# Queries and keys of two of three attention groups as block products, in a two-layer hybrid decoder on one NeuronCore

## The chip, the cores and the metric

The kernel runs on one core of one Trainium2 chip. Its time is the device time of one launch in microseconds, the median of several runs. The engines of a core work side by side, each through its own queue: TensorE (PE; its weight loads are listed apart as PEld), VectorE (DVE), ScalarE (ACT), GpSimd (POOL) and SyncE (SP), which here only issues DMAs. A change is compared with the kernel before on the same chip.

## What is computed

Two layers, each with a token mixer and an FFN, on 512 tokens of width 1024, all in float32. The mixer's input projection gives, among much else, queries, keys and values of 18 attention heads in three groups of six, with windows and dilations of their own. Cut to what matters:

```python
def _hybrid_mixer(x, rel_bias, w_in, b_in, w_attn_proj, w_ret_proj, w_out):
    z = jnp.einsum('bsd,dc->bsc', x, w_in) + b_in
    q_a, k_a, v_a, q_r, k_r, v_r, g_r, gate_a, gate_b = jnp.split(z, SPLIT_POINTS, axis=-1)
    ...
    for gi, (window, dilation) in enumerate(ATTN_GROUPS):   # (128,1), (512,4), (2048,16)
        o, lse = _dilated_window_attention(q_a[:, :, gi], k_a[:, :, gi], v_a[:, :, gi], ...)
    wts = jax.nn.softmax(jnp.stack(lses, axis=0), axis=0)
    y_a = jnp.sum(wts[..., None] * jnp.stack(outs, axis=0), axis=0)
    y_r = _retention(...)
    y_b = jax.nn.silu(g_r) * y_r
    merged = (sigmoid(gate_a) * (y_a @ w_attn_proj) + sigmoid(gate_b) * (y_b @ w_ret_proj))
    return merged @ w_out
```

The columns of `w_in` that matter here are those of q and k, 128 at a time: one column group holds two heads of one attention group.

## The kernel before

**Products.** A float32 operand is split into a high and a low part (`hilo`, or `high`/`low` in `Right`): ACT casts the loaded weights to the high part, DVE subtracts to get the low part. A product is then three matmuls (`mm3`, line 85): high by high, low by high, high by low. All matmuls of projections have line 83.

**Plain projections.** `wstat` (247) computes 128 output columns for all 512 tokens: 8 pieces of the contraction by 3 matmuls of 512 columns, with weights as the stationary operand. `pair_units` (215) loads the weights of q and k for one column group in two halves of the contraction, two DMAs each, into one raw buffer of 128 x 1024 a half; `unit` (114) makes the high and low parts.

**Block products.** `wide` (420) computes a two-by-two block product with seven products in place of eight. Columns (two output blocks), contraction and tokens are halved: product i of `ORDER` takes one block or one sum of blocks of x (`x_left`, sums S1 to S4 made once a layer) and one block or sum of blocks of the weights: B11, B12, B21, B22 and P1 = B11 + B12, P2 = P1 + B22, P3 = B12 + B22, P4 = P1 + B21. `Right` (322) loads the blocks and makes the operands: P1 and P3 are made before the change by a DMA of POOL that adds to the loaded block (`accum_op`), P2 and P4 by DVE in P1's buffer (361). The order `WIDE` is 1 (B11), 5 (P1), 6 (P2), 2 (B21), 7 (P3), 3 (B22), 4 (P4). One product is 2 x 4 x 3 = 24 matmuls of 256 columns. Results gather in three PSUM chains: A over products 1, 6, 7, 4; C over 5 and 3; X for 2. The function `ev` gets each finished chain. Rotary, the gates and the FFN use `wide`.

**Operands ahead.** Raw loads have 8 buffers, high and low parts 4 each (`wp`), PSUM 8 banks, the working tiles `w2` 6. The cast of the next product's operand is issued ahead of the present product's matmuls. Within an engine's queue the instructions are ordered at compile time by a planner that takes the next one that its model holds to be ready, in the order in which the program is written where several are; a wait that is longer in fact than in the model holds up what is queued behind it.

**Work beside.** The attention of a lot (`attention_pair`, 531) is a list of small operations: for 8 blocks `scores` (PE, then DVE and ACT for the softmax), `turn` (PE transposes, ACT copies) and `values` (PE, ACT copies), then `swap` and a tail that weighs the groups against each other. These lie in the queue `side`. `tick` (148) is called behind every three projection matmuls and takes entries from it at the rate that `pace` sets; `drain` runs what is left. `nothing` is an empty entry that sets the distance.

**The stage of the change.** Six heads a group make three lots of two heads, `hp` = 0, 1, 2 (line 900). Lot zero's queries and keys come at the layer's start. For lots one and two, lines 901 to 907 project q and k of groups 0, 1 and 2 one after the other (six `wstat`, `qk_put` on DVE adds the bias and scales), while the attention of the lot before is taken from `side` with `pace(32)`. The attention of the last lot runs beside the first rotary projection, a `wide` (line 922). In each layer the stage runs twice, so four times in all. For groups 1 and 2 the tiles `qk` are written with tokens permuted by four (`p (l r) -> p r l`).

Of the kernel before, what the change touches and what calls it, by code (L numbers as in the profile page):

```python
# [11 lines left out]
F32 = mybir.dt.float32  # L12
F32R = mybir.dt.float32r
I32 = mybir.dt.int32
AF = mybir.ActivationFunctionType
ALU = mybir.AluOpType
# [3 lines left out]
P = 128  # L20
# [5 lines left out]
HD = 64  # L26
HPG = 6
NG = 3
GW = HPG * HD
AW = NG * GW  # L30
# [7 lines left out]
C_QA, C_KA, C_VA = 0, AW, 2 * AW  # L38
# [16 lines left out]
def hybrid_kernel(ctx, tc, x, rel_bias, w_in, b_in, w_attn_proj, w_ret_proj, w_out,  # L55
                  ln1_g, ln1_b, w_ffn_gate, w_ffn_up, w_ffn_down, ln2_g, ln2_b,
                  c_cos, c_sin, c_dec, c_hot, c_id, out):
    nc = tc.nc
    pe, act, dve, pool = nc.tensor, nc.scalar, nc.vector, nc.gpsimd
# [4 lines left out]
    sm = ctx.enter_context(tc.tile_pool(name="sm", bufs=4, side="right"))  # L64
# [20 lines left out]
    def mm3(ps, ah, al, bh, bl, start, stop):  # L85
        mm(ps, ah, bh, start, False)
        mm(ps, ah, bl, False, False)
        mm(ps, al, bh, False, stop)

    def psum(name="px"):  # L90
        return psm.tile([P, S], F32, tag="mm", name=name)
# [5 lines left out]
    def raw(name="raw"):  # L97
        return rawp.tile([P, 1024], F32, tag="raw", name=name)

    def work(name):  # L100
        return wk.tile([P, S], F32, tag="w2", name=name)

    def rows(w):
        return w.rearrange("(k p) c -> p k c", p=P)

    def view(t, a, b):
        return t[:, :a * b].rearrange("p (a b) -> p a b", a=a)

    def load(src, a, b):
        v = view(raw(), a, b)  # L110
        nc.sync.dma_start(v, src)
        return v

    def unit(v):
        a, b = v.shape[1], v.shape[2]
        h = view(wp.tile([P, 1024], F32R, tag="whi", name="whi"), a, b)
        l = view(wp.tile([P, 1024], F32R, tag="wlo", name="wlo"), a, b)
        hilo(v, h, l)
        return h, l
# [26 lines left out]
    side, rate, credit, awaited = deque(), [1.0], [0.0], [0] * NI  # L146

    def tick(us):

        if side:  # L150
            credit[0] += rate[0] * us
            while side and credit[0] >= 1.0:
                credit[0] -= 1.0
                side.popleft()()

    def pace(us):
        rate[0], credit[0] = len(side) / us, 0.0

    def drain():
        while side:  # L160
            side.popleft()()
# [4 lines left out]
    def need(*tiles):  # L166

        while any(awaited[i] for i in tiles):
            side.popleft()()
# [72 lines left out]
    def part_of(us, k, q):  # L242
        h, l = us[k // 4]
        cs = slice(q * P, (q + 1) * P)
        return h[:, k % 4, cs], l[:, k % 4, cs]

    def wstat(us, q):

        need(*range(NI))
        ps = psum("ps")  # L250
        for k in range(KD):
            h, l = part_of(us, k, q)
            mm3(ps, h, l, xh[:, k], xl[:, k], k == 0, k == KD - 1)
            tick(STEP)
        return ps
# [41 lines left out]
    def tail_units(raws):  # L297

        out_ = []
        for j, r in enumerate(raws):  # L300
# [12 lines left out]
    ORDER = ((1, "A11", "B11"), (2, "A12", "B21"), (5, "S1", "P1"), (3, "S4", "B22"),  # L313
             (6, "S2", "P2"), (7, "S3", "P3"), (4, "A22", "P4"))
    CHAIN = {1: "A", 6: "A", 7: "A", 4: "A", 2: "X", 5: "C", 3: "C"}
    FIRST = (1, 2, 5)
    WIDE = tuple(ORDER[i] for i in (0, 2, 4, 1, 5, 3, 6))
    WIDE1 = tuple(ORDER[i] for i in (0, 1, 2, 4, 3, 5, 6))

    class Right:  # L320
# [1 line left out]

        def __init__(self, src, shapes, order=ORDER, loads=("B11", "B21", "P1", "P3", "B22")):
            self.src, self.shapes, self.order, self.loads, self.t = src, shapes, order, loads, {}

        def load(self, *names):
            for n in names:
                if (n, 0) in self.t:  # L330
                    continue
                for u, (a, b) in enumerate(self.shapes):
                    r = self.t[n, u] = load(self.src({"P1": "B11", "P3": "B12"}.get(n, n), u), a, b)
                    if n in ("P1", "P3"):
                        pool.dma_start(r, self.src({"P1": "B12", "P3": "B22"}[n], u), accum_op=ALU.add)  # L335
# [18 lines left out]
        def begin(self, n):  # L354

            if n == "B11":
                self.load(*self.loads)
            elif n in ("P2", "P4"):
                for u in range(len(self.shapes)):
                    r = self.t["P1", u]  # L360
                    dve.tensor_tensor(out=r, in0=r, in1=self.t["B22" if n == "P2" else "B21", u], op=ALU.add)  # L361
            return self.high(n)
# [57 lines left out]
    def wide(right, left, ev):  # L420


        ps = {}
        for (i, an, bn), ((h, l),) in zip(right.order, right.operands()):
            c = CHAIN[i]
            if i in FIRST:
                ps[c] = psum("ps")
            for q in range(2):
                cs = slice(q * P, (q + 1) * P)
                for k in range(4):  # L430
                    ah, al = left(an, k, slice(0, 256))
                    mm3(ps[c][:, q * 256:(q + 1) * 256], h[:, k, cs], l[:, k, cs], ah, al,
                        i in FIRST and q == 0 and k == 0, k == 3)
                    tick(STEP / 2)
            ev(i, ps[c])
# [217 lines left out]

    VB = 288

    bTs = []
    for ly in range(DEPTH):
        bTs.append(sm.tile([P, COLS // P], F32, tag="bT", name="bT", bufs=2))

    def bias_cols(ly, braw):  # L660
        n = COLS // P
        px = psum()
        pe.transpose(px[:, :n], braw, ident[:n, :n])
        dve.tensor_copy(bTs[ly], px[:, :n])

    def layer(ly, cp):
        w_l = rows(w_in[ly])
        b_l = b_in[ly]
        bT = bTs[ly]

        def bcol(c):
            return bT[:, c // P:c // P + 1]
# [74 lines left out]
        with stage("attn") as ap_, stage("attw", 4) as aw:  # L747
            qk = {}

            def qk_slot(hp, g):  # L750
                qk[hp, g] = opp.tile([P, 2, S], F32, tag="op", name="qk")

            def qk_units(hp, g, how=pair_units):
                c = g * GW + hp * P
                return how(w_l, C_QA + c, C_KA + c)

            def qk_put(hp, g, j, ps):
                cc = (C_QA, C_KA)[j] + g * GW + hp * P
                o_, i_ = qk[hp, g][:, j], ps
                if g:  # L760
                    o_ = o_.rearrange("p (r l) -> p r l", r=4)
                    i_ = i_.rearrange("p (l r) -> p r l", r=4)
                dve.tensor_scalar(o_, i_, bcol(cc), (HD ** -0.5, 1.0)[j], op0=ALU.add, op1=ALU.mult)

            if ly == 0:
                x0 = [slot("x0", F32) for _ in range(NI)]
# [2 lines left out]
                px = psum()  # L769
# [16 lines left out]
                for hf in range(2):  # L786
                    for i in range(2):
                        load_x(i, hf)
                    for g, j in tiles:
                        c = (C_QA, C_KA)[j] + g * GW  # L790
# [11 lines left out]
                ops = [to_xT(x0[i].rearrange("p a b -> p (a b)"), i, cp, late) for i in range(NI)]  # L802
# [52 lines left out]
            for t in range(2):  # L855
                c1, c2 = C_VA + t * VB, C_VA + (2 + t) * VB

                def put(i, s, c):
                    nc.sync.dma_start(v_d[i * P:(i + 1) * P, c - C_VA:c - C_VA + VB], s)
# [23 lines left out]
            def load_v(hp):  # L883
                v = [ap_.tile([P, NG, P], F32, tag="v", name="v", bufs=6) for _ in range(NI)]
                for i in range(NI):
                    c = hp * P
                    nc.sync.dma_start(v[i][:, 0], v_d[i * P:(i + 1) * P, c:c + P])
                    vr = v_d[:, GW:].rearrange("(l r) (g e) -> r l g e", r=4, g=2)[i]
                    nc.sync.dma_start(v[i][:, 1:], vr[:, :, c:c + P])
                return v  # L890
# [7 lines left out]
            bias, tail = {}, []  # L898
            load_bias(0)
            for hp in range(HPG // 2):  # L900
                if hp:
                    for g in range(NG):
                        us = qk_units(hp, g)
                        qk_slot(hp, g)
                        for j in range(2):
                            qk_put(hp, g, j, wstat(us, j))
                    drain()
                ops, t_ = attention_pair(hp, [qk[hp, g] for g in range(NG)], load_v(hp), outputs_last if hp == HPG // 2 - 1 else outputs_, bias, yaT)
                if hp + 1 < HPG // 2:
                    ops.insert(17, lambda hp=hp: load_bias(hp + 1))  # L910
                if hp == 0:
                    pool.dma_start(cos, c_cos)
                    pool.dma_start(sin, c_sin)
                for at, f in zip((30, 29, 27, 19, 17, 15, 13, 12, 3), reversed(tail)):
                    ops.insert(at, f)
                side.extend([nothing] * (3 if hp < 2 else 8) + ops)
                tail = t_
                pace(32)
            n = [nothing]
# [8 lines left out]
        with stage("ret") as rp:  # L928
# [57 lines left out]
            for h in range(RH):  # L986
# [7 lines left out]
                ops = ret_scores(h)  # L994
# [7 lines left out]
                ops, turns = ret_outputs(h)  # L1002
# [65 lines left out]
            for dp in range(KD // 2):  # L1068
                h, l = was[dp]
# [5 lines left out]
                for e in range(2):  # L1075
                    cs = slice(e * P, (e + 1) * P)
                    ps = psum("ps")
                    for t in range(NG):
                        mm3(ps, h[:, t, cs], l[:, t, cs], ya[t][:, 0], ya[t][:, 1], t == 0, t == NG - 1)
                    v = sgs[dp][:, e]  # L1080
# [36 lines left out]
        with stage("mp") as mp:  # L1117
# [10 lines left out]
            for dp in range(KD // 2):  # L1128
# [9 lines left out]
                for hh, (h, l) in enumerate(us):  # L1138
                    for e in range(2):
                        cs = slice(e * P, (e + 1) * P)  # L1140
                        for t in range(4):
                            k = 4 * hh + t
# [166 lines left out]
```

## Time and profile before

| | us |
|---|---|
| median of 3 runs | 2157.8 |
| lowest and highest | 2156.14, 2160.75 |
| the profiled run | 2158.48 |
| span of the profiled run, first to last instruction | 2156.7 |

The granted clock of TensorE is 0.999 over the span. The profiled run lies 0.7 us above the median, and its span 1.8 us below its time. Where the stage lies in the first layer: the last `qk_put` of lot zero is at 47.8 us, those of lot one lie between 101.0 and 144.1, those of lot two between 150.2 and 195.1; in the second layer, lots one and two lie between 1170.9 and 1265.3. All busy shares are busy time over the span, and a matmul that drains counts as busy, so starts must be compared to see TensorE's pace.

### The profile page before, as it was taken

To read this page: it belongs to the slowest core of one execution; us is meant where nothing else is said; L and a number is where in the kernel's file an instruction comes from. 1 tells how busy PE (TensorE), PEld (TensorE's weight loads), DVE (VectorE), ACT (ScalarE), POOL (GpSimd) and SP (SyncE) were. 2 spreads that over 40 slices of the span, in tenths; PEclk is the share of its full clock that TensorE was granted. 3 is DMA by queue.
4 is the path that set the end of the run, shared out by engine and by line. 5 is a ranking of instruction groups with operands and counts; after the bars stand their busy time and mean duration, and the time that the engine had idled before them with its cause. 6 is when DMAs were issued, how large, how long until landed. Compare 5 with 4: busy or idle time off the path is not lost.

```text
span 2156.7 us, 33739 instructions
## 1 busy us (share of the span) xinstructions
PE 2141.0 (99%) x13482; PEld 1896.2 (88%) x13482; DVE 1448.5 (67%) x2077; ACT 1016.2 (47%) x1573; POOL 237.9 (11%) x249
## 2 busy tenths in 40 slices
PE   9999999999999999999999999999999999999998
PEld 8977888889988899989898788888899889999996
DVE  6635897887744776747675367887867357666575
ACT  4544554655623353525245455555666233444350
POOL 5011101011000101000120111111010001010001
PEclk9999999999999999999999999999999999999999
DMA  8854458577776266656269444667777662666551
GB/s 260 241 135 102 115 146 209 157 183 176 227 266 202 63 169 145 167 128 165 72 175 250 107 112 118 155 173 192 175 187 249 229 195 59 179 144 168 123 159 39
DMA packets 317629, 351.25 MB, mean 163 GB/s; under 512 B 22173, under 2 KB 255809, under 8 KB 317344
## 3 DMA queue, kind: packets, MB, share of 16 engines
q1 hardware_dynamic: 231936, 253.01, 38.0%
q0 software_dynamic: 58256, 83.29, 21.0%
q10 hardware_dynamic: 27280, 12.80, 2.1%
q8 instruction: 105, 1.72, 0.3%
q14 instruction: 52, 0.43, 0.1%
HBM read 323.26 MB, written 28.53 MB: 163 GB/s over the span
## 4 chain that ended last, share of the span: by engine, by line
PE 92%; issue 4%; DMA 2%; DVE 1%; ACT 1%; POOL 1%; SPq 0%; POOLq 0%; DVEq 0%; ACTq 0%
PE ps L83 83%; PE px L83 7%; DMA raw<-in_w_in 1%; PE px L566 1%; PE px L974 1%; PE px L184 0%; POOL ry L126 0%; DVE xtok L1104 0%; DVE wlo L350 0%; PE px L627 0%; ACT whi L344 0%; DMA mb<-exd 0%; DVE xtok L1113 0%; DVE stats L1115 0%; ACT xh L94 0%
## 5 line engine op out<-in xcount | busy, mean ns | idle before, releaser
L350 DVE TENSOR_TENSOR wlo<-raw,whi 128x1024 fp32r<-128x1024 f32 (+1 forms) x420 | 487.2, 1162 | 240.0 <-ACT whi L344 234.1
L344 ACT CAST whi<-raw 128x1024 fp32r<-128x1024 f32 (+1 forms) x420 | 418.8, 1000 | 462.0 <-PE ps L83 268.6
L83 PE MATMUL ps<-xs,whi 128*128 128x256 f32 (+1 forms) x2560 | 500.1, 294 | 0.0
L83 PE MATMUL ps<-xh,whi 128*128 128x256 f32 (+1 forms) x1472 | 465.3, 318 | 1.7 <-ACT xh L94 1.4
L83 PE MATMUL ps<-xh,wlo 128*128 128x256 f32 (+1 forms) x1472 | 453.5, 309 | 1.0 <-DVE wlo L95 1.0
L83 PE MATMUL ps<-xl,whi 128*128 128x256 f32 (+1 forms) x1472 | 454.2, 309 | 0.0
L83 PEld LDWEIGHTS ps<-xs,whi 128*128 128x128 f32 x2560 | 408.0, 191 | 13.5 <-issue 1.7
L83 PE MATMUL ps<-xs,wlo 128*128 128x256 f32 (+1 forms) x1280 | 375.7, 294 | 0.0
L83 PEld LDWEIGHTS ps<-xh,whi 128*128 128x128 f32 x1472 | 279.5, 191 | 28.8 <-issue 10.1
L83 PEld LDWEIGHTS ps<-xh,wlo 128*128 128x128 f32 x1472 | 280.4, 191 | 15.7 <-DVE wlo L95 1.2
L83 PEld LDWEIGHTS ps<-xl,whi 128*128 128x128 f32 x1472 | 280.9, 191 | 12.5 <-DVE xl L95 0.6
L95 DVE TENSOR_TENSOR wlo<-raw,whi 128x1024 fp32r<-128x1024 f32 (+2 forms) x132 | 154.6, 1174 | 184.2 <-ACT whi L94 183.3
L83 PEld LDWEIGHTS ps<-xs,wlo 128*128 128x128 f32 x1280 | 245.0, 191 | 5.0
L94 ACT CAST whi<-raw 128x1024 fp32r<-128x1024 f32 (+2 forms) x132 | 133.0, 1011 | 227.9 <-PE ps L83 157.8
L83 PE MATMUL ps<-whi,xs 128*128 128x512 f32 (+1 forms) x768 | 225.2, 363 | 1.9 <-ACT sn L484 1.9
L83 PE MATMUL ps<-whi,ht 128*128 128x512 f32 x576 | 178.4, 389 | 0.0
L335 POOL DMA_DIRECT2D raw<-in_w_in x80 | 99.6, 1265 | 677.5 <-DMA raw<-in_w_in 274.2
L83 PEld LDWEIGHTS ps<-whi,xs 128*128 128x128 f32 x768 | 137.8, 188 | 21.6 <-ACT sn L484 2.4
L361 DVE TENSOR_TENSOR raw<-raw 128x1024 f32<-128x1024 f32 (+1 forms) x120 | 139.8, 1165 | 10.3 <-DMA raw<-in_w_in 8.1
L83 PE MATMUL ps<-wlo,xs 128*128 128x512 f32 (+1 forms) x384 | 138.3, 360 | 0.1
L83 PEld LDWEIGHTS ps<-whi,ht 128*128 128x128 f32 x576 | 108.2, 188 | 22.4
L335 POOL DMA_DIRECT2D raw<-in_w_ffn_gate x40 | 51.7, 1293 | 681.9 <-DMA raw<-in_w_ffn_up 271.8
(197 smaller groups left out, 2873.1 us busy)
## 6 DMA issues: line engine op xcount, KB each, us to landing
raw<-in_w_in SPq DMA_DIRECT2D x160, 512.0 KB, 4.9
raw<-in_w_in POOLq DMA_DIRECT2D x64, 512.0 KB, 8.2
raw<-in_w_ffn_up SPq DMA_DIRECT2D x64, 512.0 KB, 3.9
raw<-in_w_ffn_gate SPq DMA_DIRECT2D x44, 512.0 KB, 4.6
raw<-in_w_ffn_down SPq DMA_DIRECT2D x44, 512.0 KB, 3.9
raw<-in_w_ffn_gate POOLq DMA_DIRECT2D x40, 512.0 KB, 6.6
raw<-in_w_in SPq DMA_DIRECT2D x72, 256.0 KB, 4.5
raw<-in_w_ret_proj SPq DMA_DIRECT2D x32, 512.0 KB, 5.6
```

Of the source, the lines that this page charges most:

```text
L83: pe.matmul(ps, lhsT=a, rhs=b, start=start, stop=stop, skip_group_check=True)
L94: act.copy(out=hi, in_=src)
L95: dve.tensor_tensor(out=lo, in0=src, in1=hi.bitcast(F32), op=ALU.subtract)
L335: pool.dma_start(r, self.src({"P1": "B12", "P3": "B22"}[n], u), accum_op=ALU.add)
L344: act.copy(out=h, in_=src)
L350: dve.tensor_tensor(out=l, in0=src, in1=h.bitcast(F32), op=ALU.subtract)
L361: dve.tensor_tensor(out=r, in0=r, in1=self.t["B22" if n == "P2" else "B21", u], op=ALU.add)
L566: pe.transpose(px[:, hh, j * P:(j + 1) * P], s[:, hh, j * P:(j + 1) * P], ident)
L974: pe.transpose(px[:, t * P:(t + 1) * P], ys[i][:, t * P:(t + 1) * P], ident)
```

## The change

For lots one and two, groups 0 and 1 are projected together by a block product (`qk_group`): the two column blocks of a block are the two groups, the first half of the columns is q and the second k. Group 2 keeps its two `wstat` and comes first. With `adds=False`, `Right` loads B11, B12, B22 and B21 and makes all four sums on DVE; P1 has a raw buffer without a DMA, P3 is made in B12's. The result is written to the `qk` tiles by ACT, two outputs for each of four finished blocks, with the bias added; for q the bias is scaled beforehand (`bQs`, one small ACT operation a layer). `load` splits a source of two column pieces into two DMAs. The three `qk` tiles are taken before the projections, and lot one's attention starts after five empty entries in place of three.

```diff
     def load(src, a, b):
         v = view(raw(), a, b)
-        nc.sync.dma_start(v, src)
+        for v_, s_ in pieces(v, src):
+            nc.sync.dma_start(v_, s_)
         return v
+
+    def pieces(v, src):
+
+        if len(src.shape) == 3:
+            return [(v, src)]
+        n = src.shape[3]
+        return [(v[:, :, g * n:(g + 1) * n], src[:, :, g]) for g in range(src.shape[2])]
...
                 for u, (a, b) in enumerate(self.shapes):
+                    if n == "P1" and not self.adds:
+                        self.t[n, u] = view(raw(), a, b)
+                        continue
...
             if n == "B11":
                 self.load(*self.loads)
+            elif n in ("P1", "P3") and not self.adds:
+                for u in range(len(self.shapes)):
+                    if n == "P3":
+                        self.t[n, u] = self.t["B12", u]
+                    dve.tensor_tensor(out=self.t[n, u], in0=self.t["B12", u], in1=self.t["B11" if n == "P1" else "B22", u], op=ALU.add)
...
         dve.tensor_copy(bTs[ly], px[:, :n])
+        act.mul(out=bQs[ly], in_=px[:, C_QA // P:C_QA // P + NQ], mul=HD ** -0.5)
...
+            def qk_group(hp):
+
+                def src(b, u):
+                    k = 4 if b[1] == "2" else 0
+                    c = (C_KA if b[2] == "2" else C_QA) + hp * P
+                    return w_l[:, k:k + 4, c:c + 2 * GW].rearrange("p k (g c) -> p k g c", g=2)[:, :, :, :P]
+
+                sn = {}
+
+                def put(v, j, half):
+                    for g in range(2):
+                        bs = (bQs[ly], bT)[j]
+                        c = (0, C_KA // P)[j] + (g * GW + hp * P) // P
+                        o_, i_ = qk[hp, g][:, j], v[:, g]
+                        if g:
+                            o_ = o_.rearrange("p (r l) -> p r l", r=4)[:, :, half * 64:half * 64 + 64]
+                            i_ = i_.rearrange("p (l r) -> p r l", r=4)
+                        else:
+                            o_ = o_[:, half * 256:half * 256 + 256]
+                        act.activation(out=o_, in_=i_, func=AF.Identity, bias=bs[:, c:c + 1], scale=(HD ** -0.5, 1.0)[j])
+
+                def ev(i, ps):
+                    p2 = ps.rearrange("p (q t) -> p q t", q=2)
+                    if i in (1, 5, 6):
+                        sn[i] = view(work("sn"), 2, 256)
+                        act.copy(out=sn[i], in_=p2)
+                    elif i == 2:
+                        dve.tensor_tensor(out=sn[1], in0=p2, in1=sn[1], op=ALU.add)
+                        put(sn[1], 0, 0)
+                    elif i == 3:
+                        dve.tensor_tensor(out=sn[6], in0=p2, in1=sn[6], op=ALU.subtract)
+                        put(sn[6], 1, 0)
+                    elif i == 7:
+                        dve.tensor_tensor(out=sn[5], in0=sn[5], in1=p2, op=ALU.subtract)
+                        put(sn[5], 1, 1)
+                    elif i == 4:
+                        put(p2, 0, 1)
+
+                wide(Right(src, [(4, 256)], WIDE, ("B11", "B12", "P1", "B22", "B21"), False), x_left, ev)
...
             for hp in range(HPG // 2):
                 if hp:
                     for g in range(NG):
+                        qk_slot(hp, g)
+                    for g in range(2, NG):
                         us = qk_units(hp, g)
-                        qk_slot(hp, g)
                         for j in range(2):
                             qk_put(hp, g, j, wstat(us, j))
+                    qk_group(hp)
                     drain()
...
-                side.extend([nothing] * (3 if hp < 2 else 8) + ops)
+                side.extend([nothing] * (3, 5, 8)[hp] + ops)
```

More of the change, by code (lines that the diff above doesn't have):

```diff
@@ L320, in hybrid_kernel, with __init__ @@
     class Right:
-        def __init__(self, src, shapes, order=ORDER, loads=("B11", "B21", "P1", "P3", "B22")):
-            self.src, self.shapes, self.order, self.loads, self.t = src, shapes, order, loads, {}
+        def __init__(self, src, shapes, order=ORDER, loads=("B11", "B21", "P1", "P3", "B22"), adds=True):
+            self.src, self.shapes, self.order, self.loads, self.adds, self.t = src, shapes, order, loads, adds, {}
         def load(self, *names):
@@ L654, in hybrid_kernel @@
     VB = 288
-    bTs = []
+    NQ = AW // P
+    bTs, bQs = [], []
     for ly in range(DEPTH):
+        bQs.append(sm.tile([P, NQ], F32, tag="bQ", name="bQ", bufs=2))
         bTs.append(sm.tile([P, COLS // P], F32, tag="bT", name="bT", bufs=2))
```

## The prediction

> **What bounds the kernel now.** I read the page from the top: the busy shares, then the chain of work that ended last.
>
> ```profile
> span 2156.7 us, 33739 instructions
> ...
> PE 2141.0 (99%) x13482; PEld 1896.2 (88%) x13482; DVE 1448.5 (67%) x2077; ACT 1016.2 (47%) x1573; POOL 237.9 (11%) x249
> ...
> PE 92%; issue 4%; DMA 2%; DVE 1%; ACT 1%; POOL 1%; SPq 0%; POOLq 0%; DVEq 0%; ACTq 0%
> ```
>
> TensorE (PE) is busy for 99% of the span and makes 92% of the chain. VectorE (DVE) has a third of its time free, ScalarE (ACT) half. But a share over the whole span says little about a stage, so the next view is that of windows: the query and key stages of lots one and two in the first layer (lines 901 to 907), behind them the first rotary stage, which is the nearest thing to the new work, since it too makes block products with attention beside them. Columns: window and length, busy time and count by engine, granted clock, share and rate of the DMA engines.
>
> ```profile
> 92.50:143.60 51.10, 51.10 (x299) 37.12 (x298) 21.29 (x55) 22.70 (x61) 5.89 (x8) 1.00 0.76 197
> 143.60:194.60 51.00, 51.00 (x299) 36.81 (x298) 22.99 (x58) 21.64 (x58) 1.55 (x2) 1.00 0.25 63
> 194.60:225.20 30.60, 30.60 (x256) 26.59 (x255) 22.63 (x51) 19.29 (x48) 5.39 (x5) 1.00 0.74 173
> ```
>
> In all three PE has no gap, at full clock, while DVE and ACT work 21 to 23 us in the 51. The view of waits for 92 to 226 us (total, times, longest) has no row of a matmul; weight loads wait, the projections' for nothing the profile shows, the attention's now and then for ACT, each less than 0.5 us:
>
> ```profile
> PEld ps L83 <- issue: 5.9, 27, 0.3
> ...
> PEld px L83 <- ACT s L557: 1.8, 5, 0.4
> ```
>
> So these stages last as long as PE's instructions take to issue, and the change is worth what it takes from that sum, unless another engine becomes late.
>
> **The price of a matmul.** A row's second number (busy, or a mean) contains the pipeline's latency; what counts is the distance from one start to the next, read in the timeline. Projections of 512 columns in the stage, with a break for attention:
>
> ```profile
> 146.59 0.39 PE L83 MATMUL ps<-xh,whi 128*128 128x512 f32 x1
> 146.82 0.39 PE L83 MATMUL ps<-xl,whi 128*128 128x512 f32 x1
> 147.04 0.39 PE L83 MATMUL ps<-xh,wlo 128*128 128x512 f32 x1
> 147.36 0.49 PE L83 MATMUL px<-qk 64*128 64x128 f32 x4
> 147.78 0.50 PE L83 MATMUL ps<-xh,whi 128*128 128x512 f32 x1
> 148.12 0.39 PE L83 MATMUL ps<-xl,whi 128*128 128x512 f32 x1
> ```
>
> Block products of 256 columns in the rotary stage, again with a break:
>
> ```profile
> 195.42 0.28 PE L83 MATMUL ps<-xl,whi 128*128 128x256 f32 x1
> 195.54 0.28 PE L83 MATMUL ps<-xh,wlo 128*128 128x256 f32 x1
> 195.66 0.28 PE L83 MATMUL ps<-xh,whi 128*128 128x256 f32 x1
> ...
> 199.50 0.28 PE L83 MATMUL ps<-xs,wlo 128*128 128x256 f32 x1
> 199.71 0.49 PE L83 MATMUL px<-qk 64*128 64x128 f32 x4
> 200.13 0.50 PE L83 MATMUL ps<-xs,whi 128*128 128x256 f32 x2
> 200.47 0.27 PE L83 MATMUL ps<-xs,wlo 128*128 128x256 f32 x1
> ```
>
> Steady: (147.04 - 146.59)/2 = 0.225 us at 512 columns and 0.12 us at 256. Over many, in windows of the FFN, the first of 256 columns only, the second of 512:
>
> ```profile
> 840.00:890.00 50.00, 50.00 (x419) 50.00 (x418) 37.78 (x41) 26.81 (x34) 5.12 (x4) 1.00 0.69 169
> 600.00:700.00 100.00, 100.00 (x443) 82.84 (x442) 42.33 (x46) 28.00 (x30) 2.67 (x2) 1.00 0.69 221
> ```
>
> A window counts the two or so that are still draining at its start: 50/417 = 0.120 and 100/441 = 0.227 us. Half the columns cost 0.53 of the time, so a block product wins 1 - 7/8 in multiplications and loses 6% of it back. A break costs, beyond the attention's own matmuls, (0.32 - 0.227) + (0.34 - 0.227) = 0.206 us among 512s, and (0.21 - 0.12) + (0.34 - 0.24) = 0.19 us among 256s.
>
> **The sum on PE.** The diff turns, in each of four stages (lots one and two, two layers), four products of 24 matmuls with 512 columns into seven of 24 with 256. Removed: 96 x 0.227 = 21.8 us. Added: 168 x 0.120 = 20.2 us. Difference 1.6 us. Some 18 of a stage's 25 breaks now fall among 256s: 18 x 0.016 = 0.3 us. Together 1.9 us a stage, **7.5 us in all**. Group three keeps its form and only goes first.
>
> [...]
>
> **What moves to ACT and DVE.** Means of one, VectorE's groups by form and then ScalarE's:
>
> ```profile
> L350 DVE TENSOR_TENSOR wlo<-raw,whi 128x1024 fp32r<-128x1024 f32 x364 | 445.3, 1225 | 217.1 <-ACT whi L344 211.5 <-PE px L83 5.0
> L361 DVE TENSOR_TENSOR raw<-raw 128x1024 f32<-128x1024 f32 x104 | 127.7, 1228 | 1.8
> L763 DVE TENSOR_SCALAR qk<-ps,bT 128x512 f32<-128x512 f32 x36 | 26.9, 750 | 38.5 <-PE ps L83 37.7
> L1038 DVE TENSOR_TENSOR sn<-ps,sn 128x512 f32<-128x512 f32 x8 | 5.5, 687 | 2.5 <-PE ps L83 2.5
> L636 DVE TENSOR_TENSOR yaT<-yaT,y 128x512 f32<-128x512 f32 x6 | 6.5, 1085 | 0.0
> ```
>
> ```profile
> L344 ACT CAST whi<-raw 128x1024 fp32r<-128x1024 f32 x364 | 380.9, 1050 | 412.7 <-PE ps L83 231.3 <-issue 103.1 <-DVE raw L361 48.3
> L567 ACT COPY sT<-px 128x512 f32<-128x512 f32 x42 | 24.6, 586 | 29.3 <-PE px L566 29.1
> L1030 ACT ACTIVATE sb<-sn,bT 128x256 f32<-128x256 f32 x32 | 14.5, 500 | 3.5 <-DVE sn L1044 2.0 <-DVE sn L1041 1.4
> ```
>
> ACT loses 4 casts (4.2 us) and gains 7 casts (7.4), 3 copies at 0.59 (1.8) and 8 biased outputs at 0.50 (4.0): +9 us a stage. Half of those outputs write or read a permuted tile, which no ACT row shows; it costs nothing on DVE at L763, and L636, the dearest permuted row, takes 1085 against 687 ns, so 0.50 to 0.79 us; I take 0.50, since the same permutation stands at L763. DVE loses 4 subtractions (4.9) and 4 evictions (3.0), gains 7 subtractions (8.6), 4 sums of weights at 1.228 (4.9) and 3 at 0.69 (2.1): +7.7 us. A stage then has about 31 us on each of them in 49. Within the 32 us of the products alone I count two thirds of the attention's share: ACT (22 - 6.3) x 0.66 + 13.2 = 24 us, 74%; DVE (23 - 11.8) x 0.66 + 15.6 = 23 us, 72%. The rotary stage carries 74% on DVE and 63% on ACT without a gap on PE. That cover is why I cost this at little: 0.7 us in all four stages, bounds 0 and 4, the latter one cast's length (1.05) a stage. If the cover is gone, rival one gives the price.
>
> **Queues and order.** SP issues as many loads as before: 12 pieces of 256 KB a stage. With P1's empty tile seven of eight raw buffers are held, six before; but the second stage moves 63 GB/s at a DMA share of 0.25, and group three's 48 matmuls (11 us and breaks) run while the blocks land. POOL gets nothing, since the sums of weights don't go through it here. In PSUM three chains are open during the fourth product; counting the ticks, a score there finds five attention banks taken with its own, 5 + 3 = 8, all of them, none too few. Ticks: 16 x 0.68 + 56 x 0.34 = 29.9 us against a pace of 32, so two to three of the last entries run in the drain: once a last values matmul, else copies and a combination; PE goes on with the next group's weights. The two scaled biases are two small ACT copies in all. The first scores of the second lot come two entries later, which covers the last product's two ACT outputs (1 us).
>
> **Rivals.** *One, the other side: ScalarE late between turn and values.* This is the closest pair: two list entries, some 1.4 us of ticks and two breaks of 0.42 us (147.36 to 147.78), in which the copy at 0.586 must end. If it finds both a cast (1.05) and two outputs (1.0) ahead of it, it is done 2.6 us after the turn and PE stands for 0.5 to 0.9 us. It decides when over half of the pairs meet both: at 5.5 of 8 pairs beside the products, 0.75 x 5.5 x 4 = 16 us, and the time is 2157.8 - 7.5 + 16 = 2166. Against it: the rotary stage has two entries between them too, only 1.2 us of ticks at its pace (70 entries in 42 us), and no gap. For it: ACT at 74% is more than any row shows here.
>
> *Two, half the gain is lost.* P2 is made in P1's own tile, so its sum, cast and subtraction (1.23 + 1.05 + 1.22 = 3.5 us) follow P1's subtraction, while a product lasts 24 x 0.12 = 2.9 us plus breaks. If the four operand buffers don't allow the lead, each stage loses 0.6 to 1.5 us, or rival one strikes a quarter of the pairs: 2154 to 2158, which is the same time.
>
> *Three, the weight load sets the pace.* A load takes 0.19 us, by this row of the weight loads by form:
>
> ```profile
> L83 PEld LDWEIGHTS ps<-xs,whi 128*128 128x128 f32 x2560 | 408.0, 191 | 13.5 <-issue 1.7
> ```
>
> If each matmul waited for its own, 168 x 0.191 = 32 us would stand against 21.8, 4 x 10.3 = 41 us more, about 2199. The 0.120 us above exclude it. [...]
>
> **The numbers.** Made against the profiled run: its span 2156.7, its time 2158.48, the median 2157.8, so 1.1 us between span and median. 2157.8 - 7.5 + 0.7 = **2151.0 us**. A difference of over 0.2%, 4.3 us, can be told from none. Forecast 0.66 (2147.5 to 2153.5: all of the 7.5 and switch costs, or the upper bound of stalls); rival two 0.24; rival one 0.09; rival three 0.01. The low end is the full gain, 2150, less 2.5 for shorter waits ahead of the attention and for the spread of single runs. The range to 2158 takes in rival two and leaves rival one out. Faster 0.66, same 0.24, slower 0.10.
>
> **What would show it.** Right: PE's windows of the four stages shrink from 51 to about 49 us, still without gaps; 168 starts 0.12 us apart; ACT near 31 us in each. Wrong: PE waiting for ACT's sT before the values matmuls (rival one), for the lower weights of P1 or P2 (rival two), or starts at 0.19 us (rival three). Loads that land late, after group three, would show as matmuls waiting for DMA through L344.

## The result and the profile after

| | us |
|---|---|
| before, median of 14 runs of the same session | 2156.99 (2156.14 to 2162.95) |
| after, median of 14 runs | 2166.18 (2161.78 to 2171.33) |
| after over before | 1.0039, 95% interval 1.0029 to 1.0048 |
| the profiled run of after, and its span | 2161.78, 2160.0 |

The changed kernel is 0.4% slower, 9.2 us, where 6.8 us less was forecast. The page of after has these lines:

```profile
span 2160.0 us, 34404 instructions
...
PE 2134.5 (99%) x13770; PEld 1913.0 (89%) x13770; DVE 1475.8 (68%) x2101; ACT 1046.5 (48%) x1631; POOL 239.7 (11%) x249
...
PE 91%; issue 4%; DMA 2%; DVE 1%; ACT 1%; POOL 1%; SPq 0%; POOLq 0%; ACTq 0%; DVEq 0%
```

TensorE has 288 matmuls more, 4 x (168 - 96), and is busy 6.5 us less, yet the span grew by 3.3 us. So the work did shrink, and something put gaps between it. The windows of the two query and key stages and of the first rotary stage, layer one:

```profile
92.00:144.00 52.00, 49.29 (x370) 41.56 (x369) 30.78 (x56) 30.89 (x72) 4.65 (x7) 1.00 0.61 166
144.00:192.00 48.00, 45.19 (x328) 36.99 (x328) 20.85 (x55) 25.78 (x67) 2.71 (x3) 0.96 0.47 112
192.00:222.00 30.00, 29.25 (x244) 25.90 (x245) 21.62 (x46) 19.52 (x46) 5.62 (x5) 1.00 0.63 130
```

PE, without a gap before, now stands still 2.7, 2.8 and 0.8 us in them, and in the second window the granted clock is 0.96. VectorE and ScalarE work 31 us in the first window, as the sum had it, but only 21 and 26 us in the second. The view of waits, of PE alone (total, times, longest), names whom it waited for. After:

```profile
PE ps L83 <- DVE sn L508: 5.5, 2, 2.8
PE px L83 <- ACT sT L584: 3.8, 2, 2.8
...
PE px L583 <- ACT s L574: 0.7, 1, 0.7
```

Before, none of these rows is there. Three waits of the old view, 3.9 us together, lie at the start of the kernel and near 744, 1081 to 1094 and 1814 us, outside the stages of the change, and stay (DVE `warm`, ACT `xh`, DVE `wlo`, 1.5, 1.4 and 1.0 us). One more, for the value projection's evictions, falls to 0.9 us; before, it was:

```profile
PE ps L83 <- ACT sn L484: 1.9, 2, 1.4
```

**The first gap** lies at the end of the value projection, ahead of the stage of the change, at 94.3 us and again at 1166 us in layer two. PE and then DVE in the timeline (start, length; in brackets the idle time before, and what ended it):

```profile
94.25 0.29 PE L83 MATMUL ps<-whi,xl 128*128 128x288 f32 x1
97.25 0.40 PE L83 MATMUL ps<-whi,xh 128*128 128x288 f32 x1 [2.71 <-DVE sn L508]
```

```profile
91.46 0.45 DVE L508 TENSOR_TENSOR sn<-sn,ps 128x288 f32<-128x288 f32 x1
95.60 1.22 DVE L374 TENSOR_TENSOR raw<-raw 128x1024 f32<-128x1024 f32 x1 [3.70 <-DMA raw<-in_w_in]
96.75 0.45 DVE L508 TENSOR_TENSOR sn<-sn,ps 128x288 f32<-128x288 f32 x1
```

L374 is the new sum P1 = B12 + B11 of a product that PE reaches at 118.4 us, some 23 us later. It stands in VectorE's queue between the last two evictions of the value projection (L508), waits 3.7 us for its weights to land, and only then comes the eviction that PE needs. That the planner took it for ready work of an idle engine is inferred from its place. The weights were just being asked for; SP's row of these loads:

```profile
86.92 5.52 SPq L112 DMA_DIRECT2D raw<-in_w_in  x6
```

**The second gap** is at 157.7 us, in lot two's stage. ACT, then PE:

```profile
153.66 0.38 ACTq L627 DMA_DIRECT2D exd<-wb  x1
...
159.07 0.34 ACTq L631 DMA_DIRECT2D fa<-exd  x1
159.46 0.51 ACT L574 ACTIVATE s<-s,nm 128x256 f32<-128x256 f32 x1 [4.50 <-DMA exd<-wb]
...
160.46 0.35 ACT L584 COPY sT<-px 128x256 f32<-128x256 f32 x1
```

```profile
157.65 0.40 PE L83 MATMUL ps<-xh,wlo 128*128 128x512 f32 x1
160.86 0.69 PE L83 MATMUL px<-sT,v 128*64 128x128 f32 x4 [2.81 <-ACT sT L584]
161.48 0.80 PE L83 MATMUL ps<-xh,whi 128*128 128x512 f32 x1
162.08 0.63 PE L83 MATMUL ps<-xl,whi 128*128 128x512 f32 x1
162.50 0.63 PE L83 MATMUL ps<-xh,wlo 128*128 128x512 f32 x1
```

Lot zero's softmax weights go to DRAM and come back in the other token order. ACT issues both DMAs, and the second (L631, `weighed`) must not start before the first has landed, so ACT's queue stands from 154.9 to 159.1 us. Behind it are the exponentials and the copy `sT` of lot one, for which PE waits. ACT is not full there, it is held. Before the change the same wait was there, and as long, but at the quiet end of the stage, where the next thing on ACT was a cast ahead of need:

```profile
146.90 1.05 ACT L94 CAST whi<-raw 128x1024 fp32r<-128x1024 f32 x1 [4.71 <-DMA exd<-wb]
```

**The clock** is the third part. After the second gap the 512-column matmuls start 0.42 us apart (162.08 to 162.50) in place of 0.227, and the granted clock of the window says why:

```profile
160.00:165.00 5.00, 4.14 (x18) 2.99 (x20) 2.61 (x3) 3.88 (x12) 0.00 (x0) 0.66 0.01 1
```

From 161 to 164 us alone it is 0.50. A granted clock of 0.66 over 5 us is, by estimate, 1.7 us lost (0.34 x 5). The 14 runs of after spread from 2161.78 us at a mean clock of 0.998 to 2171.33 at 0.994; over them all, time follows the clock with a correlation of -0.92 and 2.2 us for each 0.001, which is what 0.001 of 2160 us comes to. The profiled run is the one that lost least, so the profile shows 3.3 us of the 9.2.

### The profile page after: what moved, and what is told of

Its sections match the earlier page's. It is cut to its first block, busy times and chain, and to the rows that moved or that the text cites. A ratio compares the mean times of both kernels' runs of the same rounds, so it can differ in the third digit from the quotient of the medians.

```text
span 2160.0 us, 34404 instructions
## 1 busy us (share of the span) xinstructions
PE 2134.5 (99%) x13770; PEld 1913.0 (89%) x13770; DVE 1475.8 (68%) x2101; ACT 1046.5 (48%) x1631; POOL 239.7 (11%) x249
## 4 chain that ended last, share of the span: by engine, by line
PE 91%; issue 4%; DMA 2%; DVE 1%; ACT 1%; POOL 1%; SPq 0%; POOLq 0%; ACTq 0%; DVEq 0%
PE ps L83 82%; PE px L83 7%; PE px L583 1%; DMA exd<-wb 1%; DMA raw<-in_w_in 1%; PE px L1036 1%; PE px L192 0%; POOL ry L134 0%; DMA mb<-exd 0%; ACT whi L356 0%; DVE xtok L1166 0%; PE px L644 0%; DVE wlo L362 0%; DMA raw<-in_w_ffn_gate 0%; DMA v_d<-sn 0%
## 5 line engine op out<-in xcount | busy, mean ns | idle before, releaser
L362 DVE TENSOR_TENSOR wlo<-raw,whi 128x1024 fp32r<-128x1024 f32 (+1 forms) x448 | 521.8, 1167 | 268.7 <-ACT whi L356 261.3
L356 ACT CAST whi<-raw 128x1024 fp32r<-128x1024 f32 (+1 forms) x448 | 447.4, 1001 | 468.6 <-PE ps L83 266.5
L83 PE MATMUL ps<-xs,whi 128*128 128x256 f32 (+1 forms) x2816 | 552.2, 295 | 0.0
L83 PEld LDWEIGHTS ps<-xs,whi 128*128 128x128 f32 x2816 | 447.1, 191 | 18.2 <-issue 5.1
L83 PE MATMUL ps<-xh,whi 128*128 128x256 f32 (+1 forms) x1440 | 438.2, 306 | 1.7 <-ACT xh L94 1.4
L83 PE MATMUL ps<-xh,wlo 128*128 128x256 f32 (+1 forms) x1440 | 430.1, 300 | 1.0 <-DVE wlo L95 1.0
L83 PE MATMUL ps<-xl,whi 128*128 128x256 f32 (+1 forms) x1440 | 431.1, 300 | 0.0
L83 PE MATMUL ps<-xs,wlo 128*128 128x256 f32 (+1 forms) x1408 | 411.7, 292 | 0.0
L83 PEld LDWEIGHTS ps<-xs,wlo 128*128 128x128 f32 x1408 | 269.3, 191 | 5.0
L95 DVE TENSOR_TENSOR wlo<-raw,whi 128x1024 fp32r<-128x1024 f32 (+2 forms) x116 | 134.9, 1166 | 162.9 <-ACT whi L94 162.8
```

Of the source, the lines that this page charges most:

```text
L83: pe.matmul(ps, lhsT=a, rhs=b, start=start, stop=stop, skip_group_check=True)
L95: dve.tensor_tensor(out=lo, in0=src, in1=hi.bitcast(F32), op=ALU.subtract)
L356: act.copy(out=h, in_=src)
L362: dve.tensor_tensor(out=l, in0=src, in1=h.bitcast(F32), op=ALU.subtract)
```

## Experiments

The theory, called Q: each gap is the head of an in-order queue (DVE, ACT) that waits for a DMA, while PE needs what is behind it; the block products themselves are worth what was forecast. Rivals: L, the blocks' loads are late whatever the order; A, ScalarE is too full, the prediction's rival one. The kernel before ran beside them on the same chip: 2158.93 us (17 runs) beside the first four, 2158.81 (15 runs) beside the others. The ratios are to it.

**e1_hold: the sums wait their turn.**

```diff
-dve.tensor_tensor(out=self.t[n, u], in0=self.t["B12", u], ...)
+with tc.issue_after(self.hold): dve.tensor_tensor(out=self.t[n, u], in0=self.t["B12", u], ...)
...
+puts = [qk_put(hp, g, j, wstat(us, j)) for j in range(2)]
-qk_group(hp)
+qk_group(hp, puts[0].ins)
```

> VectorE's sums P1 and P3 are queued behind the eviction of group two's queries; nothing else is edited. Theory Q (each PE gap is the head of an in-order queue that waits for a DMA): the gaps of 2.9 us at the end of the value projection go in both layers, 5.8 us of span, and with them part of the lost clock, so some 2158 to 2161 us against 2166; the gaps at 157 and 1229 us (3.0 and 1.2) stay. Rival L (the block's loads are late whatever the order): PE waits as long, only later, at group three's or the first block products: 2164 to 2167. Rival A (ScalarE too full): no change, about 2166.

Measured: 2152.69 us, ratio 0.9970 (0.9959 to 0.9981). The two gaps of 2.9 us are gone, and nothing waits later for the blocks (PE's only new waits for weights, 0.7 and 0.3 us, lie at 80 and 10 us, ahead of the stage): rival L falls. The time is below the expected 2158 to 2161, since the second gap went too, which had not been expected: there is no wait for `sT` left in the view, and ACT's wait shows as less, mostly in the rotary stage:

```profile
PE px L583 <- ACT s L574: 2.5, 3, 1.9
```

The granted clock of its runs is 0.997 to 0.999.

**e2_swapq: the returning DMA on another queue.**

```diff
-            act.dma_start(fa[:, 1], exd2.rearrange("(l r) c -> l r c", r=4))
+            nc.sync.dma_start(fa[:, 1], exd2.rearrange("(l r) c -> l r c", r=4))
```

> The DMA that brings the weights of the second token order back (line 631) is issued by SP in place of ACT; nothing else is edited. Theory Q: ACT no longer stands 4.5 us ahead of the scores' exponentials, so the gaps at 157, 210 and 1229 us (3.0, 0.9, 1.2) go, the two of 2.9 us stay: 2159 to 2162 us. Rival A: ACT's own work is what the values wait for, so the gaps stay within 1 us: about 2166.

Measured: 2159.03 us, ratio 0.9999 (0.9989 to 1.0009), so it takes back the 0.4% that after had lost, and no more. All of PE's waits for ACT in the attention are gone, with the same work on ACT (busy 1046.9 us, 1046.5 in after): rival A falls. The first gap stays:

```profile
PE ps L83 <- DVE sn L508: 4.6, 2, 3.0
```

**e3_both: both edits.**

> Both edits. Theory Q: all 10.9 us of gaps go, granted clock back to 0.999, so the prediction's 2151 us come out, 2149 to 2153. Rival L: 2156 to 2162. Rival A: 2160 or more.

Measured: 2149.72 us, ratio 0.9958 (0.9945 to 0.9971). The change is now 0.42% faster than the kernel before. The first line of the page, and all of PE's waits:

```profile
span 2147.5 us, 34391 instructions
```

```profile
PE px L83 <- DVE warm L828: 1.5, 1, 1.5
PE ps L83 <- ACT xh L94: 1.4, 4, 0.7
PE ps L83 <- ACT sn L501: 1.1, 1, 1.1
PE ps L83 <- DVE wlo L95: 1.0, 1, 1.0
```

None of them lies in the stages of the change. In VectorE's timeline the last eviction comes when PE has finished, and the sum stands ten microseconds behind it:

```profile
93.43 0.45 DVE L508 TENSOR_TENSOR sn<-sn,ps 128x288 f32<-128x288 f32 x1 [1.08 <-PE ps L83]
...
103.43 1.22 DVE L374 TENSOR_TENSOR raw<-raw 128x1024 f32<-128x1024 f32 x1
```

The span is 9.2 us below that of before. The waits in the views explain 0.8 of it (1.9 to 1.1 for the evictions), which leaves 8.4 for the matmuls, against 7.5 in the sum. A second reading takes PE's starts alone: from the first matmul of 512 columns behind the value projection to the first of the `px<-rot` matmuls behind the rotary projection it is 163.3 and 163.5 us before, in layers one and two, and 159.1 and 158.7 us in e3_both. That is 9.0 us less, with no wait of PE for another engine in between in either kernel.

**e4_inplace: P1 in B11's buffer.** The sum must then follow B11's own subtraction, and the stage holds six raw buffers, as before the change.

```diff
-                    if n == "P1" and not self.adds:
-                        self.t[n, u] = view(raw(), a, b)
-                        continue
...
-                    if n == "P3":
-                        self.t[n, u] = self.t["B12", u]
+                    self.t[n, u] = self.t["B11" if n == "P1" else "B12", u]
...
-("B11", "B12", "P1", "B22", "B21")
+("B11", "B12", "B22", "B21")
```

> P1 is made in B11's raw buffer in place of an empty one, so the sum must follow B11's subtraction and the stage holds six raw buffers as before the change. Theory Q: the sum can no longer stand ahead of the value projection's last eviction, so at least what e1_hold gives, 2156 to 2161; if the loads that come in a burst at 145 us collide with the exchange of the softmax sums, they now come earlier and the gap at 157 us shrinks too. Rival L: PE waits for P1 at its product, 2164 or more.

Measured: 2151.65 us, ratio 0.9963 (0.9949 to 0.9977), below the expected 2156 to 2161. Without any rule of order the data dependence keeps the sum in its place. The wait for `sT` is gone too, and the loads suggest why. In after, loads go in a burst just when the softmax sums are exchanged; here the burst lies earlier, at 135 to 140 us (share 0.99), and `mb` takes 4.2 us from issue to use in place of 8.1. The window of 145 to 150 us, after and then e4_inplace, whose last two numbers are the share of the DMA engines and the rate:

```profile
145.00:150.00 5.00, 5.00 (x29) 4.04 (x28) 0.00 (x0) 1.94 (x4) 0.00 (x0) 1.00 1.15 293
```

```profile
145.00:150.00 5.00, 5.00 (x28) 3.62 (x28) 2.50 (x10) 0.88 (x4) 0.00 (x0) 1.00 0.59 85
```

In that burst VectorE stood idle for its half of the exchange, in after:

```profile
150.24 0.17 DVE L618 TENSOR_TENSOR mn<-nm,mb 128x8 f32<-128x8 f32 x1 [6.96 <-DMA mb<-exd]
```

Before the change the same instruction waited 1.58 us. e4_inplace changes the buffers and the order of the sum at once, but e1_hold changes the order alone and keeps the seven buffers, and there it waits 1.47 us:

```profile
142.78 0.17 DVE L618 TENSOR_TENSOR mn<-nm,mb 128x8 f32<-128x8 f32 x1 [1.47 <-DMA mb<-exd]
```

In e1_hold the transfer of `mb` is issued as far ahead of lot one's first scores as in after (8.5 us), but the share of the DMA engines is 0.23 in that window of 5 us and rises to 0.96 only in the next. In e2_swapq and e6_poolsum, where the shares beside it are 0.97 and 0.81, the instruction waits 6.9 us again. So the exchange is late where loads fall on it, and later is where lot one's exponentials are. That the burst is the cause is argued from these rows and not tested by itself; the seven buffers do not bring it about alone, and what sets the time of the burst stays open.

**e5_inplace_swapq: both remedies of another kind.** e4_inplace with e2_swapq's line.

> P1 in B11's raw buffer and the returning weights' DMA on SP: the candidate for a version that beats both. Theory Q: e4_inplace kept gaps of 0.8 us at 202 and 1266 us, where scores' exponentials stand behind ACT's wait; they go, so 1.6 us less than e4_inplace: 2148 to 2151 us. If SP's wait holds up loads instead, PE waits for weights at rotary's products: 2153 or more.

Measured: 2151.29 us, ratio 0.9967 (0.9955 to 0.9980), just above the expected 2148 to 2151; its profiled span is 2146.7. The two waits of 0.7 us go, as expected, but the median does not tell it from e4_inplace, or clearly from e3_both. SP's own wait costs no visible load.

**b_swapq: the control.** The line of e2_swapq in the kernel before.

> The kernel before with the returning weights' DMA on SP, a control. Theory Q: before the change ACT's wait of 4.7 us stood where no exponential was due, so nothing is won: within 1.5 us of before. If the move itself is a gain of its own, it is 3 us or more faster, and e2_swapq and e3_both owe that to it and not to the change's gap.

Measured: 2158.36 us, ratio 1.0001 (0.9992 to 1.0010). Moving the DMA wins nothing where ACT's wait was harmless. What e2_swapq wins is the change's own gap.

**e6_poolsum: P1 and P3 by accumulating DMAs**, as the other block products have them.

```diff
-                        pool.dma_start(r, self.src({"P1": "B12", "P3": "B22"}[n], u), accum_op=ALU.add)
+                        for v_, s_ in pieces(r, self.src({"P1": "B12", "P3": "B22"}[n], u)): pool.dma_start(v_, s_, accum_op=ALU.add)
...
-("B11", "B12", "P1", "B22", "B21"), False)
+("B11", "P1", "B22", "P3", "B21"))
```

> The changed kernel with P1 and P3 made by accumulating DMAs, as the other block products do; P2 and P4 stay on VectorE. Theory Q: no sum of raw blocks can stand ahead of the value projection's last eviction, so the gaps of 2.9 us go, the gaps from ACT's wait stay, and 512 KB more are loaded twice over in each stage: 2153 to 2162 us. If it is the block products as such that lose (ACT too full, loads too late), 2164 or more.

Measured: 2172.93 us, ratio 1.0068 (1.0054 to 1.0082): a miss, and slower than after. The gap at L508 is gone, but the wait for the DMA moved from VectorE's queue to ScalarE's: the cast of P1 stands 9.9 us for the accumulating transfer, and lot zero's exponentials stand behind it. ACT's timeline, and PE's waits:

```profile
106.44 1.05 ACT L356 CAST whi<-raw 128x1024 fp32r<-128x1024 f32 x1 [9.91 <-DMA raw<-in_w_in]
```

```profile
PE px L583 <- ACT s L574: 8.9, 3, 5.1
PE px L83 <- ACT sT L584: 5.1, 2, 3.7
```

By the expectation's own sign, 2164 or more, this would speak for block products that lose as such. For these accumulating transfers it does: they land too late. For block products in general it does not, since e3_both makes the same seven products and is faster than before. So the sum on VectorE is the better of the two; the expectation rested on loads in time.

**e7_three: e3_both with three empty entries.**

```diff
-                side.extend([nothing] * (3, 5, 8)[hp] + ops)
+                side.extend([nothing] * (3, 3, 8)[hp] + ops)
```

> e3_both with three empty entries ahead of lot one's attention in place of five, as before the change. If the distance covers the last product's two ACT outputs, the first scores wait for them: up to 1 us a layer, 2150 to 2153. If not, within 1 us of e3_both, about 2150.

Measured: 2149.51 us, ratio 0.9958 (0.9943 to 0.9974). The two entries make no difference that can be told.

## Why the prediction was wrong

- **The price of the matmuls was about right, and a little low.** 7.5 us were forecast (the printed terms give 7.6), and the busy time of PE fell by 6.5 us in after, part of it at a lower clock (0.998 over the span of after, 0.999 before); with the queues put right, e3_both ran 8.4 to 9.0 us shorter beside the waits.
- **The work on ACT and DVE was sized nearly right.** Four times 9 and 7.7 us more were forecast, 36 and 31; the busy times of the whole kernel grew by 30.3 and 27.3 us. Rival one, ScalarE late because it is full, came out in its place, `sT` ahead of the values, but not by its mechanism: e2_swapq took the wait away and left ACT's work. That its price, 2166 us, is the time measured is chance.
- **The step that failed** is "What moves to ACT and DVE", with its "that cover is why I cost this at little: 0.7 us", bounds 0 and 4. It weighed added instructions by their length alone. A sum of raw blocks is also a wait: it is VectorE's first instruction in the stage to depend on two loads and no cast. No instruction was named that would stand behind it, and behind it stood the value projection's last eviction: 2.9 us in each layer. In place of the 0.7 us, PE's new waits are 10.0 us (5.5, 3.8 and 0.7). "Queues and order" went by the same rule, saying that group three's 11 us would cover the landing of the blocks. They cover it for PE, and e1_hold shows that; they don't cover it for VectorE's queue, in which the sum was put ahead of the stage.
- **The second miss** is in "Queues and order": "seven of eight raw buffers are held, six before; but the second stage moves 63 GB/s at a DMA share of 0.25". The share of a whole stage hides bursts; in after one of 293 GB/s over 5 us fell on the exchange of softmax sums. ACT's standing wait of 4.7 us was in the trace of before, unseen in the prediction because no PE row named it.
- **What was missing altogether** is the clock. The bounds priced a gap at its length; the clock added some 2.2 us for each 0.001 over the runs. As a rough estimate, 8.4 us less for the matmuls, 9.0 more in waits (10.0 new, 1.0 less at the evictions) and 6.6 for a clock of 0.996, the median of the 14 runs, in place of 0.999 give 7 us more; 9.2 were measured, with an interval of 6.3 to 10.4.

## What to carry to other kernels

When work moves onto an engine that takes its queue in order, ask of each instruction what it waits for and what stands behind it, not only how long it takes: in after a sum of 1.22 us waited 3.7 us for its load, and PE 2.7 us for the eviction behind it. An operation that reads a load directly belongs behind the evictions that come before it, by a rule of order or by a data dependence such as an in-place sum; here the ratio to before fell from 1.0039 to 0.9970 with the first (e1_hold) and to 0.9963 with the second (e4_inplace). A wait that costs nothing now can be a price when the work around it moves: ACT's of 4.71 us held up nothing on PE before, and its 4.50 us in after held up PE for 2.8. So read the waits of the other engines too, where PE has none. A gap on PE of some 3 us can cost more than itself: behind that of 2.8 us at 157.7 us the granted clock was 0.66 over 5 us, an estimated 1.7 us more.

## What had not been expected of the hardware

The mean granted clock of the runs of after, whose profile has gaps of up to 2.8 us on PE, lies between 0.994 and 0.998, that of e3_both's runs, whose longest wait of PE in the profile is 1.5 us, at 0.998 to 0.999. Of three gaps about equally long in the profile of after, those at 94.3 and 1166 us (2.71 and 2.77 us) left the clock at 1.00, from 94 to 104 us and from 1166 to 1172 us, and that at 157.7 us (2.81) was followed by starts 0.42 us apart at a clock of 0.50. In e2_swapq the first gap, 3.0 us there, was followed by half the clock from 97 to 103 us, of which one window:

```profile
98.00:99.00 1.00, 1.00 (x6) 1.00 (x6) 1.00 (x2) 0.00 (x0) 0.00 (x0) 0.50 1.00 284
```

The 0.42 us are 1.85 times the 0.227 us measured at a clock of 1.00. After gaps of 2.7 to 3.0 us the clock fell in some places and not in others. Why stays open.

A small exchange through DRAM took 2 us or 8 us from issue to use: `mb` was issued at 136.82 and used at 138.83 before, issued at 142.11 and used at 150.24 in after, 140.14 and 142.78 in e1_hold. The share of the DMA engines was 0.21 from 136.8 to 138.8 us before and 1.07 from 142.1 to 150.2 us in after.
